# A hybrid attention and mLSTM step: the loads and the order of work ahead of the first projections

## The chip, the cores and the metric

The kernel runs on one core of a Trainium2 chip. The metric is the device time of one execution in microseconds (us), the median of several runs. In what follows PE is the tensor engine (PEld its weight loads), DVE the vector engine, ACT the scalar engine, POOL GpSimd, and SP the sync engine, which here only issues transfers (DMAs).

## The reference

One layer of a diffusion backbone. There are 128 context tokens and 1024 latent tokens, nine blocks of 128, of width 1024, all in float32. Cut to what matters here:

```python
def ada_mods(cond, w_ada_l, b_ada_l):
    m = jax.nn.silu(cond) @ w_ada_l + b_ada_l          # w_ada: 1024 x 6144
    return jnp.split(m.reshape(-1, 1, 6 * D_MODEL), 6, axis=-1)

def trunk_layer(x, mods, norm1_w, w_in, ...):
    sh1, sc1, g1, sh2, sc2, g2 = mods
    h = rmsnorm(x, norm1_w) * (1 + sc1) + sh1
    aq, ak, av, mq, mk, mv, mo, mg = jnp.split(h @ w_in, SPLIT_POINTS, axis=-1)
    ...                                                # attention beside mLSTM
    x = x + g1 * mix
    h2 = rmsnorm(x, norm2_w) * (1 + sc2) + sh2
    x = x + g2 * swiglu(h2, w_gu, w_down)
```

Context tokens are modulated by one condition vector, latent tokens by another. `w_in` is 1024 x 2832: its columns 512 to 767 give keys and values (`ak`, `av`), its last 16 the mLSTM gates (`mg`), columns 0 to 511 the queries.

## The kernel before

A Tile program: it is written as one sequence per part, and a scheduler settles at build time the order of the instructions on each engine from priorities (`hot(n)` raises them) and from its own estimate of times. Each engine then runs its instructions strictly in that order, and an instruction that waits holds up everything behind it on its engine. Products in float32 accuracy are made from splits into a high and a low half and three products: high times high, high times low, low times high.

The nine blocks are handled three at a time, as chunks c = 0, 1, 2 (`CB` = 3, `NCH` = 3); chunk c's rows lie in `x3[c]` (in the profile `x`). The part that the change touches is the start:

- **Loads.** SP issues, in this order: the identity `ident` (L117), six blocks of x (`load_x`, L308), the key, value and gate columns of `w_in` into four tiles `kraw` (two strided pieces each, L208), the 16 tiles `aw` of the columns of `w_ada` for shift (n = 0) and scale (n = 1) (L324), the last three blocks of x, the gate bias, and the four tiles `iraw` of the query columns (L208). ACT's queue issues the small vectors `crow`, `brow`, `nrow`. Every DMA from the ninth on waits for one of the eight before it to land.
- **Normalising and turning.** `normalise(c)` takes the sums of squares on ACT (L384), the root on DVE (L131 to L137), and scales the rows on DVE (L387). `turn(c)` transposes the rows on PE (L120, by the identity) and copies them back, half on ACT (L400), half on DVE (L401).
- **The scale of a weight set.** `Scaled.ready` takes the largest magnitude of a weight set on ACT (L214, `jkw`), transposes it on PE (L120), makes a power of two of it on DVE (`powers`, L176 to L179) and spreads it over the partitions on PE (L190). `pairs` splits the scaled weights into f16 halves `ipair` (L234, L235, L237, L238).
- **Shift and scale.** For each n, products of the condition with the 8 tiles `aw[n]` go to two banks, the halves j = 0, 1 (L370). Each bank is copied (`part`, L417, j = 0 on ACT, j = 1 on DVE), turned into columns (L376) and gets its bias (`modulation`, L362, L365). From both, one more power of two is made (L426 to L431).
- **Features.** `features(c)` makes the modulated rows `hT` in f16: the high half on ACT (L536), the full value on DVE (L537, four buffers `full`), their difference on DVE (L141).
- **Projections.** `linear_tok` multiplies a chunk's features by the key/value/gate weights (L512 to L514, 128x272). `evac_kvg` takes the result out on ACT (L521, L522) and the gates on DVE (L525). For c = 1 and 2 it is woven with the scale of the query weights and `ada_rest`, the products for the remaining mods (L370 with tiles `a`). After it the queries are projected (L512 to L514, 128x512).

The loop that orders the last two is short:

```python
    for c in range(NCH):
        with hot(100):
            features(c)
        prods = linear_tok(kvg_pairs, 0, 272, evac_kvg, (tuple(range(c * CB, c * CB + CB)),), bank if c == 1 else bankA)
        if c > 0:
            weave(prods, chain(steps, ada), KD, 10)
        else:
            emit(prods)
        if c == 0:
            normalise(2)
        if c == 1:
            turn(2)
```

Two loads further down play a part in the prediction: `mwh` (L771, scaled on DVE at L772), the mLSTM norm weights, and the store of `vall` (L725). After about 160 us come the mLSTM heads, the attention, the output projection and the FFN; nothing of them is touched.

## Time and profile before

| | |
|---|---|
| time, median of 3 runs (lowest to highest) | 1531.25 us (1525.82 to 1537.16) |
| profiled execution: its time, its span | 1531.07 us, 1529.3 us |
| PE busy in the span | 1473.0 us (96%) |
| DVE, ACT, POOL busy | 1015.8, 770.4, 268.8 us |
| mean granted PE clock | 0.989 of full |
| moved by DMA | 233.77 MB, mean 153 GB/s |
| PE busy in the first 45.65 us | 26.77 us |
| PE busy from 45.65 to 100 us, and from 100 to 155 us | 48.56 and 55.00 us |

The span is the profiled program from its first to its last instruction; the execution's time is some 2 us more. "PEclk" is the share of the full clock that PE was granted. In the lines of the timeline come the start and the length in us, the engine, the line of the kernel, the operation with out<-in, and in brackets the idle time just before it and what ended it. "SPq" and "ACTq" are the issuing of DMAs on these engines.

### The profile page before, as it was taken

The page shows a single profiled execution, that of the slowest core. Times are in us where ns is not written, and L with a number is a line of the kernel's source. Part 1 is how long each engine was busy: PE and PEld are TensorE (multiplying, and loading weights), DVE is VectorE, ACT ScalarE, POOL GpSimd, SP SyncE. Part 2 cuts the span into 40 slices and gives each one's busy share as a digit, 9 for nine tenths or more (in the row PEclk, how much of TensorE's full clock was granted, in tenths as well). Part 3 has the DMA queues.
Part 4 walks back from the last instruction along what each step waited for, and adds up shares of the span by engine and source line. Part 5 has one row for each costly group of instructions (what it writes and reads, how often), then busy time and mean ns, then how long its engine had stood idle before and what let it go on. Part 6 is the DMA issues. An engine that isn't in the chain of part 4 may idle for free.

```text
span 1529.3 us, 23410 instructions
## 1 busy us (share of the span) xinstructions
PE 1473.0 (96%) x8539; PEld 1244.7 (81%) x8539; DVE 1015.8 (66%) x2025; ACT 770.4 (50%) x1429; POOL 268.8 (18%) x354
## 2 busy tenths in 40 slices
PE   6899999999998899999999999999999999999997
PEld 3545567677766789999898999989998989999996
DVE  4887654838568866878637587787866585554554
ACT  4764475947654645556433444656553443323333
POOL 0113423333344441010010100100010101101110
PEclk9899999999999999999999999999999999999998
DMA  9664323523456577869635357886864445544541
GB/s 359 205 198 147 101 71 42 120 53 62 110 177 207 135 180 187 200 156 195 171 115 166 124 184 212 198 184 145 201 145 138 138 139 179 158 135 126 153 144 56
DMA packets 387113, 233.77 MB, mean 153 GB/s; under 512 B 170102, under 2 KB 347462, under 8 KB 386998
## 3 DMA queue, kind: packets, MB, share of 16 engines
q1 hardware_dynamic: 385006, 228.69, 55.0%
q10 hardware_dynamic: 1864, 3.20, 0.9%
q8 instruction: 67, 1.10, 0.3%
q14 instruction: 48, 0.39, 0.1%
q0 software_dynamic: 128, 0.39, 0.1%
HBM read 182.21 MB, written 11.69 MB: 127 GB/s over the span
## 4 chain that ended last, share of the span: by engine, by line
PE 78%; DVE 5%; DMA 3%; ACT 3%; issue 1%; POOL 1%; SPq 0%; ACTq 0%; DVEq 0%; POOLq 0%
PE mm L1437 11%; PE mm L1436 11%; PE mm L1435 11%; PE mm L1191 5%; PE mm L1192 5%; PE mm L1193 5%; PE S L1111 4%; PE wi L514 3%; PE wi L513 3%; PE wi L512 3%; PE mm L1219 2%; PE po L1136 2%; PE po L1135 2%; PE mm L1221 2%; PE mm L1223 2%
## 5 line engine op out<-in xcount | busy, mean ns | idle before, releaser
L163 ACT CAST whi<-raw 128x1024 fp32r<-128x1024 f32 x214 | 219.2, 1026 | 367.8 <-PE mm L1436 146.9
L141 DVE TENSOR_TENSOR wlo<-raw,whi 128x1024 fp32r<-128x1024 f32 x214 | 257.7, 1204 | 170.5 <-ACT whi L163 167.0
L1436 PE MATMUL mm<-aTl,whi 128*128 128x384 f32 x1056 | 354.4, 336 | 0.0
L1437 PE MATMUL mm<-aTh,wlo 128*128 128x384 f32 x1056 | 354.2, 336 | 0.0
L1435 PE MATMUL mm<-aTh,whi 128*128 128x384 f32 x1056 | 353.2, 335 | 0.0
L141 POOL TENSOR_TENSOR hl<-tn,hl 128x384 fp32r<-128x384 f32 x66 | 84.9, 1286 | 846.6 <-ACT hl L1458 796.4
L1435 PEld LDWEIGHTS mm<-aTh,whi 128*128 128x128 f32 x1056 | 198.3, 188 | 0.7
L1436 PEld LDWEIGHTS mm<-aTl,whi 128*128 128x128 f32 x1056 | 198.3, 188 | 0.6
L1437 PEld LDWEIGHTS mm<-aTh,wlo 128*128 128x128 f32 x1056 | 198.3, 188 | 0.1
L1191 PE MATMUL mm<-whi,hl 128*128 128x512 f32 x372 | 144.4, 392 | 1.1 <-DVE t L1180 1.1
L1192 PE MATMUL mm<-wlo,hl 128*128 128x512 f32 x372 | 145.1, 391 | 0.0
L1193 PE MATMUL mm<-whi,hl 128*128 128x512 f32 x372 | 142.7, 391 | 0.0
L1118 DVE SCALAR_TENSOR_TENSOR pl<-pr,st,ph 128x1152 f16<-128x1152 f32 (+1 forms) x72 | 96.9, 1346 | 37.3 <-ACT ph L1117 35.9
L1113 DVE TENSOR_REDUCE st<-S 128x1 f32<-128x1152 f32 (+1 forms) x72 | 88.9, 1234 | 17.5 <-PE S L1111 17.2
L1114 ACT ACTIVATE pr<-S,st 128x1152 f32<-128x1152 f32 (+1 forms) x72 | 81.3, 1129 | 33.0 <-DVE st L1113 28.2
L1117 ACT ACTIVATE ph<-pr,st 128x1152 f16<-128x1152 f32 (+1 forms) x72 | 83.8, 1164 | 26.3 <-issue 10.9
L1180 DVE TENSOR_TENSOR t<-mm,gl 128x512 f32<-128x512 f32 x102 | 69.1, 686 | 38.1 <-PE mm L1193 16.0
L512 PE MATMUL wi<-headw,hT 128*128 128x384 f16 x288 | 93.9, 326 | 0.2 <-ACT th L799 0.2
L513 PE MATMUL wi<-headw,hT 128*128 128x384 f16 x288 | 93.9, 326 | 0.0
L514 PE MATMUL wi<-headw,hT 128*128 128x384 f16 x288 | 93.9, 326 | 0.0
L1111 PE MATMUL S<-kst,qT 128*128 128x384 f32 (+1 forms) x400 | 84.5, 344 | 0.8 <-ACT pr L1114 0.8
L1191 PEld LDWEIGHTS mm<-whi,hl 128*128 128x128 f32 x372 | 69.9, 188 | 15.2 <-DVE t L1180 1.5
(400 smaller groups left out, 2591.3 us busy)
## 6 DMA issues: line engine op xcount, KB each, us to landing
raw<-in_w_gu_dram SPq DMA_DIRECT2D x132, 512.0 KB
raw<-in_w_down_dram SPq DMA_DIRECT2D x60, 512.0 KB
a<-in_w_ada_dram SPq DMA_DIRECT2D x24, 512.0 KB
gl<-g_d SPq DMA_DIRECT2D x36, 256.0 KB
aw<-in_w_ada_dram SPq DMA_DIRECT2D x16, 512.0 KB
iraw<-in_w_in_dram SPq DMA_DIRECT2D x32, 256.0 KB
x<-in_x_sample_dram SPq DMA_DIRECT2D x11, 512.0 KB
raw<-in_w_out_dram SPq DMA_DIRECT2D x10, 512.0 KB
```

Of the source, the lines that this page charges most:

```text
L141: (dve if eng == "dve" else pool).tensor_tensor(out=out, in0=full, in1=hi, op=ALU.subtract)
L163: nc.scalar.copy(hi[:, :n], raw[:, :n])
L512: mm(ps[:, :n], ah, wh[:, k % 2, c0 : c0 + n], start=(k == 0), stop=False)
L513: mm(ps[:, :n], ah, wl[:, k % 2, c0 : c0 + n], start=False, stop=False)
L514: mm(ps[:, :n], al, wh[:, k % 2, c0 : c0 + n], start=False, stop=(k == KD - 1))
L1111: mm(S[:, n, 0:w], qT[:, h, :], kst[kv][:, t, c0 + n * w : c0 + (n + 1) * w], start=(t == 0), stop=(t == 1))
L1191: mm(ps, ah, wh[:, k % 2, :], start=(k == 0), stop=False)
L1192: mm(ps, ah, wl[:, k % 2, :], start=False, stop=False)
L1193: mm(ps, al, wh[:, k % 2, :], start=False, stop=(k == nk - 1))
L1435: mm(ps, wh[:, k, :], th[:, k, :], start=(k == 0), stop=False)
L1436: mm(ps, wh[:, k, :], tl[:, k, :], start=False, stop=False)
L1437: mm(ps, wl[:, k, :], th[:, k, :], start=False, stop=(k == KD - 1))
```

## The change

It makes these edits, all ahead of some 100 us of the program:

1. The identity is issued by ACT's queue, ahead of the small vectors, and no longer by SP's ahead of x.
2. The key, value and gate columns of `w_in` are packed on the host into one more input, `w_kvg`, four tiles of 128 rows of 544 numbers; each `kraw` is one DMA of whole rows.
3. The tiles `aw` for scale come in two passes, first the eight left halves, then the eight right ones: 24 DMAs in all in the place of 16.
4. For scale, each half is multiplied, copied, turned and modulated before the next is begun.
5. `normalise(2)` and `turn(2)` stand ahead of chunk 1's features, with a raised priority.
6. For chunk 1, every second full value is made on ACT (L536 there) in the place of DVE.

```diff
-    dma(ident, I["k_ident"])
+    nc.scalar.dma_start(ident, I["k_ident"])
...
-    kvg = Scaled([[(lambda v: v[:, :, 0:256], rows_of(j)[:, :, 512:768]),
-                   (lambda v: v[:, :, 256:272], rows_of(j)[:, :, 2816:2832])] for j in range(4)], (2, 272),
+    kvg = Scaled([[(lambda v: v, I["w_kvg"][j])] for j in range(4)], (2, 272),
...
-    ada_w = [[], []]
-    for n in range(2):
+    ada_w = [[awp.tile([P, D], F32, name=f"aw0_{n}_{k}") for k in range(KD)] for n in range(2)]
+    for n, j, w in ((0, 0, D), (1, 0, 512), (1, 1, 512)):
         for k in range(KD):
-            aw = awp.tile([P, D], F32, name=f"aw0_{n}_{k}")
-            dma(aw, w_ada[k * P : (k + 1) * P, n * D : (n + 1) * D])
-            ada_w[n].append(aw)
+            dma(ada_w[n][k][:, j * w : (j + 1) * w], w_ada[k * P : (k + 1) * P, n * D + j * w : n * D + (j + 1) * w])
...
         halves = [bankA(), bankA()]
-        for k in range(KD):
-            for j, pe in enumerate(halves):
-                strip_products(pe, k, silp, ada_w[n][k][:, j * 512 : (j + 1) * 512], 2 * j)
-        with hot(300):
-            for j, pe in enumerate(halves):
-                part = p0.tile([P, 512], F32, name=nm("part"), tag="part", bufs=2)
-                (nc.scalar.copy if j == 0 else dve.tensor_copy)(part, pe)
-                cols_from_strips(out, n, j, part, bankA)
+        for js in ((0, 1),) if n == 0 else ((0,), (1,)):
+            for k in range(KD):
+                for j in js:
+                    strip_products(halves[j], k, silp, ada_w[n][k][:, j * 512 : (j + 1) * 512], 2 * j)
+            with hot(300):
+                for j in js:
+                    part = p0.tile([P, 512], F32, name=nm("part"), tag="part", bufs=2)
+                    (nc.scalar.copy if j == 0 else dve.tensor_copy)(part, halves[j])
+                    cols_from_strips(out, n, j, part, bankA)
...
-                dve.tensor_scalar(out=full[:, i : i + n], in0=v[:, k, i : i + n], scalar1=s, scalar2=t, op0=ALU.mult, op1=ALU.add)
+                if c == 1 and k % 2:
+                    act(full, v[:, k], AF.Identity, scale=s, bias=t)
+                else:
+                    dve.tensor_scalar(out=full[:, i : i + n], in0=v[:, k, i : i + n], scalar1=s, scalar2=t, op0=ALU.mult, op1=ALU.add)
...
     for c in range(NCH):
+        if c == 1:
+            with hot(200):
+                normalise(2)
+                turn(2)
...
-        if c == 0:
-            normalise(2)
-        if c == 1:
-            turn(2)
...
+    w = host["w_in"][0]
+    w = _np.concatenate([w[:, 512:768], w[:, 2816:2832]], 1)
+    host["w_kvg"] = w.reshape(4, 2, P, 272).transpose(0, 2, 1, 3)
```

Three places show what this does to the order. The first is ACT's queue just ahead of the first features (`hT`), before: `part` is the copy of a half of shift or scale, `jk` the squares of chunk 2's rows, `jkw` the maxima of the query weights `iraw`.

```order
L234 ACTIVATE ipair_362<-kraw_144,isc_332 128x544
L417 COPY part_383<-wi_365 128x512
L417 COPY part_417<-wi_399 128x512
L384 ACTIVATE jk_620,ssx_619<-x_2_134 128x1024
L384 ACTIVATE jk_622,ssx_619<-x_2_134 128x1024
L384 ACTIVATE jk_624,ssx_619<-x_2_134 128x1024
L214 ACTIVATE jkw,isc_689<-iraw_476 128x512
L536 ACTIVATE hT_439<-x_0_132,shift_88,scale_87 128x128
```

And with the change:

```order
L415 COPY part_387<-wi_369 128x512
L234 ACTIVATE ipair_357<-kraw_141,isc_336 128x544
L234 ACTIVATE ipair_360<-kraw_142,isc_336 128x544
L234 ACTIVATE ipair_363<-kraw_143,isc_336 128x544
L234 ACTIVATE ipair_366<-kraw_144,isc_336 128x544
L415 COPY part_413<-wi_403 128x512
L381 ACTIVATE jk_624,ssx_623<-x_2_134 128x1024
L381 ACTIVATE jk_626,ssx_623<-x_2_134 128x1024
L381 ACTIVATE jk_628,ssx_623<-x_2_134 128x1024
L214 ACTIVATE jkw,isc_729<-iraw_480 128x512 x2
L214 ACTIVATE jkw,isc_729<-iraw_481 128x512
L534 ACTIVATE hT_443<-x_0_132,shift_88,scale_87 128x128
```

The copy of the shift half has moved ahead of the four splits of the key weights, and three maxima, one of them of the second `iraw`, stand ahead of the features where there was one.

The second place is PE after chunk 1's projections, before: `isc` and `pv` belong to the scale of the query weights, `a` to the remaining mods, `x_2` is chunk 2.

```order
L514 MATMUL mm_679<-ipair_362,hT_440 128x272
L120 MATMUL mm_726<-ident,isc_689 1x128
L190 MATMUL mm_743<-pv_728,one_110 128x2
L370 MATMUL mm_772<-a_89_755,silp_473 32x256 x4
L370 MATMUL mm_772<-a_90_757,silp_473 32x256 x4
L120 MATMUL mm_804<-ident,x_2_134 128x128 x4
L370 MATMUL mm_772<-a_91_759,silp_473 32x256 x4
L120 MATMUL mm_809<-ident,x_2_134 128x128 x4
```

With the change the same work on the scale stands at the end of chunk 2's projections:

```order
L512 MATMUL wi_878<-ipair_366,hT_445 128x272
L190 MATMUL mm_783<-pv_768,one_110 128x2
L367 MATMUL mm_812<-a_95_795,silp_477 32x256 x4
L367 MATMUL mm_812<-a_96_797,silp_477 32x256 x4
L367 MATMUL mm_812<-a_97_799,silp_477 32x256 x4
L367 MATMUL mm_812<-a_98_801,silp_477 32x256 x4
L510 LDWEIGHTS hT_443
L510 MATMUL wi_1077<-ipair_1048,hT_443 128x512
```

Chunk 2's transposes have moved into chunk 0's projections, all of chunk 2's projections come next, and the first products for the remaining mods and the queries follow the scale (its transpose L120 stands eleven projections earlier).

The third place is DVE around that scale with the change: `pv` is the scale, `rt` and `ry` the root of the key norms.

```order
L186 TENSOR_REDUCE pv_768<-mm_766 1x1
L137 SCALAR_TENSOR_TENSOR ry_1120<-rt_1121,ry_1120 128x2
L135 TENSOR_TENSOR rt_1191<-ry_1190 128x8
L176 TENSOR_SCALAR pv_768<-pv_768 1x1
L135 TENSOR_TENSOR rt_1121<-ry_1120 128x2
L136 SCALAR_TENSOR_TENSOR rt_1191<-rt_1191,rv_1189 128x8
L773 TENSOR_SCALAR mwh<-mwh 128x512
L177 TENSOR_SCALAR pv_768<-pv_768 1x1
L136 SCALAR_TENSOR_TENSOR rt_1121<-rt_1121,rv_1119 128x2
L137 SCALAR_TENSOR_TENSOR ry_1190<-rt_1191,ry_1190 128x8
L577 CAST maskb<-maskf_1095 128x128
L178 TENSOR_SCALAR pv_768<-pv_768 1x1
```

The scaling of `mwh` and a cast of a mask, which both read tiles that were loaded, have moved between the pieces of the scale.

## The prediction

> **What bounds the kernel now.** I read the busy shares first, then the span cut into stretches, then the timeline of the first hundred microseconds engine by engine, then who waits for whom.
>
> The first line of the page, and the busy time of each stretch (length, then PE, PEld, DVE, ACT and POOL busy, granted clock, share of the DMA engines, GB/s):
>
> ```profile
> PE 1473.0 (96%) x8539; PEld 1244.7 (81%) x8539; DVE 1015.8 (66%) x2025; ACT 770.4 (50%) x1429; POOL 268.8 (18%) x354
> ...
> 0.00:45.65 45.65, 26.77 (x153) 15.83 (x154) 22.34 (x88) 23.55 (x52) 1.37 (x7) 0.90 0.99 365
> 45.65:100.00 54.35, 48.56 (x350) 31.66 (x351) 48.58 (x147) 38.90 (x85) 11.01 (x11) 0.89 0.63 181
> 100.00:155.00 55.00, 55.00 (x367) 26.90 (x366) 42.90 (x164) 28.72 (x52) 14.47 (x9) 1.00 0.50 160
> 155.00:160.00 5.00, 2.86 (x19) 1.77 (x18) 3.12 (x7) 3.14 (x5) 0.00 (x0) 1.00 0.77 236
> 160.00:1529.30 1369.30, 1339.78 (x7655) 1168.50 (x7653) 898.89 (x1623) 676.11 (x1237) 241.92 (x327) 0.99 0.55 144
> ```
>
> The tensor engine sets the pace, so a gain is PE idle time removed or a clock drop avoided. All edits lie in the start: from about 100 us on, every engine's order is the same in both kernels but for small swaps before 160 us. PE is idle 18.9 us before the first projection at 45.65, 5.8 us from there to 100, nothing from 100 to 155. The first 45.65 us have a floor, since the DMA engines are busy 0.99 of them. So the stake is a few microseconds of 1529, in either direction, far inside the 1% (15 us) that a measurement of this kernel can tell from no change.
>
> What releases the first projection:
>
> ```profile
> 26.61 2.66 ACT L234 ACTIVATE ipair<-kraw,isc 128x544 f16<-128x544 f32 x4 [2.63 <-DVE isc L191]
> 29.18 0.56 ACT L417 COPY part<-wi 128x512 f32<-128x512 f32 x1
> 29.80 3.48 PE L376 MATMUL wi<-strip_sel,part 128*128 128x2 f32 x16 [2.21 <-ACT part L417]
> 33.21 5.59 PE L370 MATMUL wi<-aw,silp 128*32 128x512 f32 x32
> 39.84 1.95 PE L376 MATMUL wi<-strip_sel,part 128*128 128x2 f32 x16 [1.05 <-ACT part L417]
> 41.83 0.17 DVE L362 TENSOR_TENSOR scale<-wi,bcol 128x8 f32<-128x8 f32 x1 [0.53 <-PE wi L376]
> 43.27 0.14 DVE L176 TENSOR_SCALAR pv<-pv 1x1 f32<-1x1 f32 x1
> 44.69 0.23 DVE L431 TENSOR_SCALAR scale<-scale,hsc 128x16 f32<-128x16 f32 x1
> 45.10 11.91 ACT L536 ACTIVATE hT<-x,shift,scale 128x128 f16<-128x128 f32 x24 [0.92 <-DVE shift L431]
> 45.65 0.41 PE L512 MATMUL wi<-ipair,hT 128*128 128x272 f16 x1 [1.19 <-ACT hT L536]
> ```
>
> This is one chain: the shift part waits on ACT behind four weight splits, so the products for scale start at 33.21 instead of when their weights are there, and the two halves of scale go through copy, strip sums and modulation together before the features may start.
>
> **The change part by part.** First the stream of loads. The identity leaves the sync queue, and the gate/kv weights come as four packed rows instead of eight strided pieces:
>
> ```profile
> 0.74 0.40 SPq L117 DMA_DIRECT2D ident<-in_k_ident_dram  x1
> 1.20 0.41 SPq L308 DMA_DIRECT2D x<-in_x_prompt_dram  x1
> ...
> 10.00:18.00 8.00, 4.67 (x26) 4.29 (x28) 7.08 (x33) 7.44 (x21) 0.00 (x0) 1.00 1.06 327
> 18.00:40.00 22.00, 18.58 (x109) 8.72 (x105) 10.54 (x24) 6.92 (x15) 0.60 (x1) 0.84 1.03 407
> 40.00:45.00 5.00, 2.64 (x19) 2.28 (x19) 2.50 (x18) 3.63 (x8) 0.00 (x0) 0.86 1.04 396
> ```
>
> The first x leaves 0.46 us earlier (1.20 less 0.74). While the strided pieces are under way the engines are full and move 327 GB/s instead of 407: 8 us at 80 GB/s less is 0.64 MB, or 1.6 us. The scale weights come as sixteen 256 KB pieces with rows of 2 KB instead of eight of 512 KB; the nearest row is the iraw loads after 40 us, also 2 KB rows, at 396: 4.19 MB at 396 instead of 407 is 0.3 us more. Net the stream is 0.46 + 1.6 - 0.3, about 1.7 us, ahead. The bounds are 2.1 (no cost of the split) and -0.4 (the split runs at 327, 2.5 us more). The identity on ACT's queue delays crow by about one issue (0.4 us); the transposes that need the identity start only at 13 us, and the condition's column is due when the first ada weights are there, after 17 us, so it costs nothing; without that cover it would be 0.4.
>
> The Trainium skill ("DMA: Bandwidth & Descriptors", Measured) speaks against the split: it asks for transfers of at least 1 MiB and lists 138 GB/s at 64 KB and 341 at 1 MB. This trace disagrees for several transfers in flight, since the 512 KB pieces of 18 to 40 us ran at 407; 256 KB pieces no run here shows yet.
>
> Second, the ada chain. The shift part now stands ahead of the four splits on ACT, and scale goes in two halves. Counted back from the first iraw load, which landed at 43.46 (below), with 2.1 MB (chunk 2's x, 1.57 MB, and that load, 0.52) behind the last ada weights, these were there at 43.46 - 2.1/0.407 = 38.3; now 36.6. Only one half's tail is left: the last product 0.35, the copy 0.7, half the strip sums 1.0, and 41.83 to 44.69, 2.9: the scaled shift would be ready at 41.6 instead of 44.7. But two other queues stand in the way:
>
> ```profile
> 39.69 1.06 ACT L384 ACTIVATE jk<-x 128x1024 bf16<-128x1024 f32 x1
> ...
> 43.46 0.63 ACT L214 ACTIVATE jkw<-iraw 128x512 bf16<-128x512 f32 x1 [0.55 <-DMA iraw<-in_w_in_dram]
> 44.00 0.19 ACT L214 ACTIVATION_READ_ACCUMULATOR jkw<-iraw 128x1 f32 x1
> ```
>
> On ACT three of these maxima (two of the first iraw, one of the second) now stand ahead of the features, before it was one. The second iraw lands 43.46 - 1.7 + 0.52/0.407 = 43.05; the first one's two, 0.73 each, run from 41.8 to 43.2, the third to 44.0. On DVE the root for chunk 2 now stands inside the power-scale chain and waits for that chunk's squares: landed at 40.5 (43.46 - 1.7 - 1.3), squared by 41.7, then 1.9 us of chain (43.27 to 44.69 before, and three more of 0.17), then the two scalings, 0.4: 44.0 as well. So the features start at 44.0 instead of 45.10, and **the first term is 1.1 us**, not the 3.1 of the ada chain. Its bounds: -1.0 (stream at the low bound) to 3.1.
>
> Third, what follows the start. Rows of PE by stretch, and of the two kinds of work that move:
>
> ```profile
> 45.65:53.65 8.00, 6.99 (x30) 4.19 (x31) 8.00 (x27) 8.00 (x18) 0.00 (x0) 0.50 1.11 319
> 58.60:67.10 8.50, 8.50 (x74) 6.95 (x71) 8.50 (x24) 5.89 (x20) 3.31 (x3) 1.00 0.03 9
> 67.10:69.60 2.50, 0.56 (x4) 0.36 (x3) 2.43 (x20) 1.99 (x7) 0.00 (x0) 1.00 0.01 3
> 71.00:74.40 3.40, 3.40 (x23) 1.94 (x22) 1.86 (x8) 1.58 (x3) 0.87 (x2) 0.52 0.89 286
> ...
> 67.67 0.27 PE L120 MATMUL mm<-ident,isc 128*1 128x128 f32 x1 [0.56 <-DVE isc L216]
> 69.32 0.38 PE L190 MATMUL mm<-pv,one 1*128 1x2 f32 x2 [1.38 <-DVE pv L179]
> 74.94 1.53 PE L120 MATMUL mm<-ident,x 128*128 128x128 f32 x12
> 80.11 0.64 PE L370 MATMUL mm<-a,silp 128*32 128x256 f32 x8 [0.45 <-DMA a<-in_w_ada_dram]
> ```
>
> Before, PE runs out of work at 67.1 and waits for the scale of the q weights; the clock then falls and 71.0 to 74.4 go at 0.52, 3.4 x 0.48 = 1.6 us lost. Now chunk 2's 24 transposes lie inside chunk 0's projections, and chunk 2's 72 products run on without a break, with the scale's transpose 11 products ahead of their end. PE from 44.55: 1.5 idle (1.0 as in the first row, 0.5 for DVE's normalise now between the first features), 216 products at 8.5/72 = 0.118, 25.5; 24 transposes at 0.128, 3.1; and the half clock of the first 8 us, 4.0: 78.6. DVE and ACT keep up:
>
> ```profile
> L141 DVE TENSOR_TENSOR hT<-full,hT 128x384 f16<-128x384 f32 x16 | 9.6, 621 | 0.0
> L537 DVE TENSOR_SCALAR full<-x,scale,shift 128x384 f32<-128x384 f32 x8 | 5.1, 662 | 0.0
> L387 DVE TENSOR_SCALAR x<-x,ry 128x1024 f32<-128x1024 f32 x3 | 2.1, 739 | 0.0
> L401 DVE COPY x<-mm 128x512 f32<-128x512 f32 x3 | 2.1, 691 | 2.1 <-PE mm L120 2.0
> L235 DVE SCALAR_TENSOR_TENSOR ipair<-iraw,isc,ipair 128x1024 f16<-128x1024 f32 x2 | 2.6, 1276 | 0.4 <-ACT ipair L234 0.4
> L728 DVE TENSOR_REDUCE vm<-vall 128x1 f32<-128x1280 f32 x1 | 1.5, 1475 | 0.0
> ```
>
> DVE did chunks 0 and 1 from 44.7 to 65.5, 20.8 us without a pause. To that come chunk 2's normalise and copies, 4.0 back to back, and three of its features, 1.8; four features go over to ACT, -2.4, and 1 us of the root now lies ahead of the start. That is 23 us from 43.6: 66.8. Chunk 2's other five features, eight subtractions and the gate columns are 9 us more: 76, ahead of PE's 78.6. Then PE waits for the scale: transposed at 77.3, and behind it on DVE the six small operations of the chain with as many of the key's norm and the 128x512 mwh scaling between them, some 2.6 us: 79.9, a gap of 1.4 where it was 2.5. The 16 ada products (2.1) and four with the high part (0.9) lead to 83.3; the low part needs DVE's 1.5 (vm) and 1.2 (ipair) and is there at 84.1: 0.8. With 0.9 for what I can't place, PE's idle time is 1.5 + 1.4 + 0.8 + 0.9 = 4.6 where it was 5.8: **the second term is 1.2 us**. The gap being shorter than the one that brought the clock down, **the third term is the 1.6 us**; if it falls again the term is 0.
>
> The Trainium skill ("TensorE: Matmul & The Clock Gate", HAM oscillation) lets the clock fall only after idle gaps over about 3.4 us. The rows above show it fall after 2.5 us with 0.56 us of small matmuls in them, so the row decides here; by the page alone 1.4 us would be safe with more room.
>
> Last, whether the gain lasts. PE is full from 100 to 155 and idles 2.1 us behind one wait:
>
> ```profile
> PE wi L849 <- ACT qraw L754: 2.1, 1, 2.1
> ```
>
> The norms that lead to it start from q products that move with PE, so I carry the gain through whole. The sum is 1.1 + 1.2 + 1.6 = 3.9 us off the profiled execution, whose own time is 1531.07, 0.2 below the median of the three runs: **1527.2 us**, 0.3% faster.
>
> **The rivals.** (1) Nothing is left: DVE and ACT are full from 45 to 57 and the extra 4.0 us of chunk 2's work there delays PE, while the gap at the end of chunk 2 is as long as the old one and the clock falls too. The second term becomes -0.5 and the third 0: 1530.5. For it: 8.00 of 8.00 on both engines. Against it: chunk 2's end comes from PE's sum, not DVE's.
> (2) Slower, on one wait: the mwh scaling on DVE now lies between the pieces of the scale chain, and DVE stops there until that load lands; PE's L190 and everything behind it (ada products, all q products) stand still. It decides against the change once DVE waits over 2.3 us, since the clock's 1.6 goes too. A wait of 5 us gives 3.9 - 1.6 - 5 = 2.7 lost: 1533.8. For it: the load is issued behind the store of vall, which waits for ACT. Against it: that store was issued at 59 us, some 18 us ahead.
> (3) The split is slow after all, the rule of the page on transfer sizes, here as 4.19 MB at the strided pieces' 327 GB/s: the start is 1.0 late instead of 1.1 early: 1529.3. The 407 of the 512 KB pieces speaks against it.
> (4) More: the clock recovers sooner, PE having less idle time ahead of the features: 4.0 us more at most, 1523.2. Against it: PE still has only some 3 us of work in the last 8 ahead of them.
>
> **How the numbers follow.** I give my forecast 0.42, (1) 0.25, (2) 0.13, (3) 0.10, (4) 0.10. The time is the forecast's. The range goes from 1521 to 1535: the rivals' 1523.2 to 1533.8, and some 2 us on each side, because the runs of the kernel before alone spread from 1525.8 to 1537.2. No case reaches 1% on either side. I leave 0.03 for a gain over 1% (the idle time of the whole start would have to go), 0.04 for a loss over 1% (a wait like (2) of 17 us or more), 0.93 for within.
>
> **What would show it.** Right: the rate stays near 400 GB/s from 10 to 18 us; the first L510-L512 product (L512 to L514 now) starts near 44.6, released by ACT; ACT waits for an iraw load just ahead of its features; no clock drop after 58 us; the gap ahead of the scale's L190 is under 2 us; the order from 100 us on is 3 to 5 us earlier. Wrong: features that start at 42 (then the two queues don't gate), a second stretch at 0.5 clock near 80, a DVE wait on mwh, or a stretch from 100 to 160 us that takes back what was won.

## The result and the profile after

The changed kernel takes 1527.3 us (median of 22 runs, 1524.0 to 1530.9) against 1531.7 us (22 runs, 1525.8 to 1537.2) in the same session: the ratio is 0.9974, with a 95% interval from 0.9964 to 0.9983. That is 4.0 us less by the ratio, where 3.9 were forecast. The profiled execution took 1524.74 us with a span of 1523.0, near the low end of the 22 runs and 6.3 us less than the profiled execution before. So the size was right (by the interval, 2.6 to 5.5 us less), and 0.3% can be told from no change here, finer than the 1% that the prediction allowed a measurement. The way to it was not in all its steps.

The page's first line after, and the same stretches as before (length, then PE, PEld, DVE, ACT and POOL busy, granted clock, share of the DMA engines, GB/s):

```profile
PE 1466.2 (96%) x8539; PEld 1239.4 (81%) x8539; DVE 1017.2 (67%) x2021; ACT 771.3 (51%) x1433; POOL 268.0 (18%) x354
...
0.00:45.65 45.65, 26.25 (x153) 14.19 (x153) 22.80 (x95) 24.35 (x55) 1.31 (x7) 0.94 0.97 363
45.65:100.00 54.35, 49.39 (x370) 32.16 (x371) 46.87 (x150) 42.82 (x92) 12.90 (x12) 0.95 0.60 172
100.00:155.00 55.00, 53.11 (x364) 26.50 (x362) 46.19 (x155) 28.17 (x52) 12.76 (x8) 1.00 0.61 193
155.00:160.00 5.00, 5.00 (x34) 3.09 (x31) 4.74 (x13) 4.86 (x14) 0.00 (x0) 1.00 0.51 158
...
70.00:75.00 5.00, 5.00 (x46) 4.23 (x44) 5.00 (x16) 3.17 (x11) 0.05 (x1) 1.00 0.02 5
```

From 45.65 to 100 us PE is busy 49.39 instead of 48.56 us, and at 0.95 of the clock instead of 0.89; the stretch near 70 us, at 0.52 before, now runs at full clock. From 100 to 155 PE idles 1.9 us where it idled nothing, and from 155 to 160 it idles nothing where it idled 2.1. In the first 45.65 us nothing was won. The timeline there:

```profile
38.87 1.06 ACT L381 ACTIVATE jk<-x 128x1024 bf16<-128x1024 f32 x1 [5.01 <-DMA x<-in_x_sample_dram]
...
40.72 0.17 DVE L362 TENSOR_TENSOR scale<-scale,ncol 128x8 f32<-128x8 f32 x1
...
42.78 0.17 DVE L131 TENSOR_SCALAR rv<-ssx 128x3 f32<-128x3 f32 x1 [0.85 <-ACT jk L381]
...
43.30 0.63 ACT L214 ACTIVATE jkw<-iraw 128x512 bf16<-128x512 f32 x1 [0.55 <-DMA iraw<-in_w_in_dram]
...
44.67 0.34 DVE L538 TENSOR_SCALAR full<-x,scale,shift 128x128 f32<-128x128 f32 x1
...
45.44 1.85 ACT L534 ACTIVATE hT<-x,shift,scale 128x128 f16<-128x128 f32 x4
45.97 0.41 PE L510 MATMUL wi<-ipair,hT 128*128 128x272 f16 x1 [2.03 <-ACT hT L534]
```

The two queues hold the features up as foreseen: DVE's root (L131) waits for chunk 2's squares, and ACT goes through three maxima before its first feature. But the first iraw lands at 43.30, only 0.16 us ahead of the 43.46 before, so the first projection is at 45.97, 0.3 us later than before and 1.4 later than forecast. The first of the head products, an order that both kernels share, shows what is left of it all:

```profile
L849 PE MATMUL wi<-hT,headw x96: 322/326/336, 158.2 to 381.6; 128*128 128x384 f16 x96
```

before, and after:

```profile
L850 PE MATMUL wi<-hT,headw x96: 323/326/336, 153.3 to 376.6; 128*128 128x384 f16 x96
```

It starts 4.9 us earlier and ends 5.0 us earlier. The other 1.3 us of the profiled 6.3 arose later, in work that the change doesn't touch. The likely reason, not tested, is the clock: 13 of the 14 executions profiled here have one to three drops of it between 270 and 530 us, and this one has none.

### The profile page after: what moved, and what is told of

Its sections match the earlier page's. It is cut to its first block, busy times and chain, and to the rows that moved or that the text cites. A ratio compares the mean times of both kernels' runs of the same rounds, so it can differ in the third digit from the quotient of the medians.

```text
span 1523.0 us, 23411 instructions
## 1 busy us (share of the span) xinstructions
PE 1466.2 (96%) x8539; PEld 1239.4 (81%) x8539; DVE 1017.2 (67%) x2021; ACT 771.3 (51%) x1433; POOL 268.0 (18%) x354
## 4 chain that ended last, share of the span: by engine, by line
PE 59%; DVE 2%; DMA 1%; ACT 0%; issue 0%; SPq 0%; DVEq 0%
PE mm L1438 11%; PE mm L1437 11%; PE mm L1436 11%; PE mm L1192 5%; PE mm L1193 5%; PE mm L1194 5%; PE S L1112 3%; PE po L1137 1%; PE po L1136 1%; DMA plT<-pl 1%; PE mm L1224 1%; PE mm L1220 1%; PE mm L1222 1%; DVE t L1181 0%; DVE x L1182 0%; PE mm L120 0%
```

## The experiments

Ratios are to the kernel before, measured beside it. Each interval is about 0.0013 wide to either side (2 us), so two kernels that differ by 2 us are not quite told apart (the interval of such a difference is 2 to 3 us to either side); the traces carry more than the times.

**The load stream alone.**

```diff
# on the kernel before
+    nc.scalar.dma_start(ident, I["k_ident"])            # was dma(...)
+    kvg = Scaled([[(lambda v: v, I["w_kvg"][j])] ...    # packed on the host
```

> The kernel before with edits 1 and 2 alone: the identity on ACT's queue, the key, value and gate weights packed. By the prediction's first term the stream is 2.1 us ahead: 393 GB/s or more from 10 to 18 us, the last of the scale weights landing near 36.2 instead of 38.3, the second modulation at 39.8 instead of 41.8. Four maxima of iraw stand ahead of the features here, so they start when the second iraw tile has landed and been read, 44.0 to 44.4, and the first projection near 44.8 instead of 45.65. Chunk 2 is still transposed behind chunk 1, so the idle stretch ahead of the query scale and the clock drop near 70 us stay as in the kernel before if the drop is a matter of that gap. Time: 0.8 below the kernel before (1530.9), at most 2.1 below. If the stream is not ahead in the end because something later takes it back (the rival), the second modulation is at 41 or later and the time that of before.

Measured: 1531.03 us, ratio 1.0003 (0.9992 to 1.0014). Two stretches of its stream:

```profile
24.00:34.00 10.00, 9.63 (x63) 4.39 (x63) 5.22 (x16) 3.83 (x6) 0.00 (x0) 0.83 1.03 407
...
38.50:41.00 2.50, 1.95 (x16) 1.86 (x16) 0.72 (x5) 2.50 (x6) 0.00 (x0) 0.98 1.06 405
```

and of its timeline:

```profile
40.74 0.17 DVE L364 TENSOR_TENSOR scale<-scale,ncol 128x8 f32<-128x8 f32 x1
...
41.56 0.63 ACT L214 ACTIVATE jkw<-iraw 128x512 bf16<-128x512 f32 x1
...
45.04 0.41 PE L511 MATMUL wi<-ipair,hT 128*128 128x272 f16 x1 [1.19 <-ACT hT L535]
```

The same two stretches of the changed kernel:

```profile
24.00:34.00 10.00, 8.58 (x56) 4.20 (x56) 5.21 (x15) 4.42 (x7) 0.00 (x0) 0.83 1.05 385
38.50:41.00 2.50, 1.20 (x9) 0.97 (x8) 1.19 (x5) 2.05 (x3) 0.00 (x0) 1.00 0.72 223
```

The packing does what the first term said: the second modulation is done 1.3 us earlier than before (40.74 for 42.03), the first iraw is read at 41.56 instead of 43.46, the first projection starts 0.6 us earlier. In the changed kernel that lead is lost again: 385 instead of 407 GB/s over 10 us (0.5 us), and a hole at 38.5 to 41 us, 223 instead of 405 (1.1 us). And a lead at the start brought no time by itself.

What was expected further down did not come. Chunk 2 is still turned behind chunk 1, but the gap ahead of the products that follow the query scale is only 1.0 us, and the clock does not fall near 70 us:

```profile
69.78 1.89 PE L369 MATMUL mm<-a,silp 128*32 128x256 f32 x26 [0.97 <-DVE isc L191]
```

So this kernel starts 0.6 us earlier and has no drop near 70 us, and still its time is that of the kernel before. This bears on the third term of the prediction (below).

**Whole loads for scale, and the gate on ACT.** The first kernel puts ACT's maxima behind the features, the second also loads the scale weights whole again.

```diff
         with hot(100):
             features(c)
+            if c == 0:
+                nc.scalar.copy(jkw[:, 0:1], hTh[0][:, KD - 1, 0:1])
```

```diff
# the second one also
-    for n, j, w in ((0, 0, D), (1, 0, 512), (1, 1, 512)):
+    for n, j, w in ((0, 0, D), (1, 0, D)):
```

> The changed kernel with one small ACT copy into the maxima's scratch tile behind chunk 0's last feature, so that ACT's maxima of the query weights all stand behind the features. Theory G (the gate on ACT set the start): the features start when DVE has scaled shift and scale, which was 44.5 us in the changed kernel, so the first projection starts near 45.0 instead of 45.97, and since that microsecond lies in the stretch at half clock the time falls by 0.5 to 1.0 us against the changed kernel, to about 1526.6. Theory S (the stream of loads set it, through chunk 2's x, whose squares stand ahead of the features on ACT and whose root stands inside DVE's chain): the features start at 44.4 to 44.7 and no earlier, since DVE still waits for the squares at 42.8. If the first projection stays at 45.9, both are wrong. In either case the transpose and the gap ahead of the query scale stay at 1 to 2 us.

> As the kernel before it in this list, and the scale weights come whole again, eight loads of 512 KB instead of sixteen of 256 KB (their products still go half by half). Theory S: the stretch from 24 to 34 us runs at 405 to 410 GB/s instead of 383, worth 0.6 us, the hole from 38.5 to 41 us (113 to 256 GB/s, worth 1.1 us) closes, and the last iraw load lands 1 to 1.7 us earlier; chunk 2's squares end near 41.3 and DVE scales near 43.2. Rival (the split cost nothing; the hole is that of the gate bias's 64-byte rows and stays): the stretch stays at 383 to 390 and the squares end at 42.4 or later. The products of scale's left half can't start before all weights of both halves are there, so the second modulation may be no earlier than 40.5. Sixteen transposes of chunk 2 stand ahead of the first projection in this order, so the first projection is late by up to 2 us and tells nothing by itself. Time within 2 us of the changed kernel's, 1525 to 1529.

Measured: 1528.94 us, ratio 0.9990 (0.9979 to 1.0001), and 1530.75 us, ratio 1.0001 (0.9990 to 1.0013). Both miss. Of the first, what PE waited for:

```profile
PE mm L190 <- DVE ry L137: 5.1, 1, 5.1
```

(us in total, times, the longest), and of its stretches:

```profile
80.00:85.00 5.00, 1.28 (x10) 0.90 (x14) 4.27 (x24) 0.49 (x1) 1.12 (x2) 0.77 0.27 66
```

The first projection did not come earlier (46.26), because in this execution PE ran at half clock from 31.5 to 52 us and the ada chain with it; and the maxima, once behind, ran so late that the query scale kept PE waiting 5.1 us and the clock fell. So the maxima ahead of the features were no loss on balance: they pay for the short gap later. In the second, the stream ran at 407 GB/s in both stretches, as with whole loads in the kernel above: the halves go with the lower rate, and the deep hole was seen only with them. Its order of transposes was another one and its time tells nothing more.

**The gate bias.**

```diff
-    dma(gbias, ...)          # ahead of the iraw loads
     next(steps)              # issues the iraw loads
+    dma(gbias, ...)
```

> The changed kernel with one load moved: the gate bias (128 rows of 64 bytes) is issued behind the four iraw loads instead of ahead of them; every other order stays. In the kernels with halved scale loads the stream showed a hole from 38.5 to 41 us (113 to 290 GB/s) while those small rows went through, in the kernels with whole loads it didn't (405). Theory S (the hole is these rows meeting a queue that holds too little): the rate stays near 400 from 38.5 to 41, the first iraw lands near 42.2 instead of 43.3, the third x before 40.5, ACT's maxima end a microsecond sooner and the first projection starts near 45.0 instead of 45.97; time 1526.3 to 1526.8. Rival (the hole comes from the halves alone): it stays where it is, first projection at 45.9, time 1527.3.

Measured: 1526.49 us, ratio 0.9972 (0.9957 to 0.9987). In its stretches:

```profile
38.50:41.00 2.50, 1.61 (x11) 0.58 (x3) 0.77 (x2) 2.21 (x5) 0.00 (x0) 0.50 1.04 406
...
30.45:54.35 23.90, 17.88 (x78) 9.30 (x73) 13.72 (x56) 14.90 (x33) 0.00 (x0) 0.50 0.98 339
```

and in its timeline:

```profile
41.51 0.63 ACT L214 ACTIVATE jkw<-iraw 128x512 bf16<-128x512 f32 x1
...
42.52 0.17 DVE L362 TENSOR_TENSOR scale<-scale,ncol 128x8 f32<-128x8 f32 x1
...
45.71 0.34 DVE L538 TENSOR_SCALAR full<-x,scale,shift 128x128 f32<-128x128 f32 x1
...
80.41 0.35 PE L190 MATMUL mm<-pv,one 1*128 1x2 f32 x2 [1.33 <-DVE rt L135]
```

The hole is gone (406 GB/s), and the maxima start at 41.51: with the halves, it was the 128 rows of 64 bytes of the gate bias that made it. Why they cost more behind the smaller loads, no run here shows. The features start no earlier all the same: scale is ready only at 42.52, because PE ran at half clock from 30.45 to 54.35 us. The time came out as expected, but the first projection did not (46.24 instead of 45.0), and the time isn't told apart from the changed kernel's, so the agreement says little.

**The clock.** What separates these executions shows in one kernel's rows. The changed kernel:

```profile
33.48:43.72 10.24, 6.26 (x35) 3.01 (x35) 2.95 (x18) 4.24 (x8) 0.00 (x0) 1.00 0.96 358
43.72:50.54 6.82, 4.48 (x20) 2.48 (x20) 6.75 (x29) 6.76 (x18) 0.00 (x0) 0.50 1.08 370
```

Half clock comes in multiples of 3.41 us, from 3.4 to 23.9 us in these executions, on a grid that lies elsewhere in each. Up to the features the order of work is nearly the same in nine of the profiled kernels. In five of them the clock stayed at half from 30 to 31.5 us on until 47.7 or later; in four it was back by 33.5 or 38.4, or had not fallen before 43. In the first group scale is ready at 42.1 to 42.6 us, in the second at 39.9 to 40.7. In four of the nine, the changed kernel and those without edit 5, without edit 6 and with the maxima behind, the loads and the order of PE's products up to the first projection are the same, one for one; two of them fell in each group. So it is the execution and not the edit that decides, and the ada chain loses or wins some 2 us by it. The Trainium skill ("TensorE: Matmul & The Clock Gate", What's actually happening) says that the activity window is 3413 ns long and free-running, so that the number of slow products varies from run to run; these traces agree, with pieces of 3.41 us and its multiples.

**Holding the clock.**

```diff
+    filler(3, "strip")       # 128x128 by 128x272 products, read by nobody
     ...
+        filler(5, "turned")
     ...
+        filler(8, "spread")
```

> The changed kernel with sixteen extra products on PE whose results nobody reads (128x128 by 128x272, f16): three behind the strip sums of scale's second half, five behind the transpose of the bound, eight behind the spread of its power, all in time in which PE idled (40.3 to 46 us). Every other order stays. Theory C (PE's clock falls after 43 us because PE has so little to do from 40 to 46, and the length of that half clock is what separates fast from slow executions): the half clock after 43 us shrinks from 6.8 to 13.7 us to at most 3.4, and since each 3.4 us of it holds 1.6 to 1.7 us of lost work the time falls by 1.5 to 3 us, to 1524.3 to 1525.8. Rival D (DVE, busy 5.00 of 5 us from 45 to 85, sets the pace of the features in this stretch, so a faster PE only waits more): PE's waits for hT on DVE grow by what the clock gives, and the time stays within 0.5 us of 1527.3. If the extra products don't hold the clock, nothing moves either, but the clock shows it.

Measured: 1528.2 us, ratio 0.9980 (0.9967 to 0.9993). In its stretches:

```profile
30.59:47.66 17.07, 14.98 (x67) 7.72 (x61) 7.20 (x39) 8.38 (x19) 0.00 (x0) 0.50 1.03 378
...
55.00:60.00 5.00, 3.55 (x28) 2.44 (x26) 5.00 (x8) 4.77 (x10) 4.70 (x5) 1.00 0.42 87
```

and in its timeline:

```profile
45.72 0.34 DVE L550 TENSOR_SCALAR full<-x,scale,shift 128x128 f32<-128x128 f32 x1
...
80.42 0.35 PE L190 MATMUL mm<-pv,one 1*128 1x2 f32 x2 [1.33 <-DVE rt L135]
```

In the kernel with the later gate bias, the stretch to set beside it:

```profile
55.00:60.00 5.00, 5.00 (x46) 4.45 (x45) 5.00 (x8) 4.77 (x10) 4.71 (x5) 1.00 0.41 90
```

Its time was not the 1524.3 to 1525.8 of theory C; it is 0.9 us above the 1527.3 of rival D, within the interval. The traces say more, and this is the clearest pair of the study. Both kernels start their features on DVE at 45.7. In one the clock is back at 47.7, in the other at 54.35, 6.7 us later; and yet the query scale is spread at 80.42 in the one and 80.41 in the other, released by DVE in both. What the clock gave, PE spent waiting for DVE (1.45 us idle from 55 to 60). That is what rival D (theory D from here on) says: DVE, which pauses for 0.1 us at most from 45 to 85, sets the pace up to there. In the changed kernel the distance from DVE's first full value to that product is the same: 79.21 less 44.67 is 34.5, here 34.7 twice. The row of that product in the changed kernel:

```profile
79.21 0.35 PE L190 MATMUL mm<-pv,one 1*128 1x2 f32 x2 [1.33 <-DVE rt L135]
```

**Chunk 1's full values back on DVE, and chunk 2 back in its old place.**

```diff
# the first: without edit 6
-                if c == 1 and k % 2:
-                    act(full, v[:, k], AF.Identity, scale=s, bias=t)
-                else:
                     dve.tensor_scalar(out=full[:, i : i + n], ...
```

```diff
# the second: without edit 5
-        if c == 1:
-            with hot(200):
-                normalise(2)
-                turn(2)
...
+        if c == 0:
+            normalise(2)
+        if c == 1:
+            turn(2)
```

> The changed kernel without edit 6: the four full values of chunk 1 that ACT made are DVE's again, 4 x 0.6 = 2.4 us more on DVE between 55 and 75 us. By the prediction's sum (DVE would be done at 76 against PE's 78.6 with the edit) PE's end moves by nothing to 0.5 us, since DVE ends at about the same time as PE then: 1527.3 to 1527.8. Rival D (DVE sets the pace from 45 to 85 us already): the whole 2.4 us show up at the end of chunk 2's projections, 77.9 becomes about 80, and the time is 1529.0 to 1529.7.

> The changed kernel without edit 5: chunk 2 is normalised behind chunk 0's projections and turned behind chunk 1's, as before. If terms two and three are what edit 5 brought, PE again runs dry behind chunk 1's projections ahead of the query scale (2 us or more with only small products in it), the clock may fall to half for 3.4 us near 70 us, and the time is 1.2 to 2.8 us above the changed kernel's: 1528.5 to 1530.1. Rival (the gain is the half clock at the start being shorter, and has nothing to do with edit 5): the time stays at 1527.3 and the half clock after 45 us lasts to about 50.5 here too.

Measured: 1528.07 us, ratio 0.9986 (0.9974 to 0.9997), and 1529.65 us, ratio 0.9988 (0.9976 to 1.0000). Of the first:

```profile
43.86 0.34 DVE L535 TENSOR_SCALAR full<-x,scale,shift 128x128 f32<-128x128 f32 x1
...
80.22 0.38 PE L190 MATMUL mm<-pv,one 1*128 1x2 f32 x2
```

The distance is 36.4 instead of 34.5 to 34.7 (PE, held up by the features on the way, comes to that product without a wait): 1.7 to 1.8 of the 2.4 us of work show on the path, most of what theory D says, and not the 0 to 0.5 of the prediction's sum. The time lies between the two forecasts. By the ratios, edit 6 is worth 1.8 us and edit 5 2.1, each with an interval of some 2.3 us to either side, so neither is told from nothing by the times alone. Without edit 5 the clock drops again, from 61.9 to 65.3 us:

```profile
60.00:65.00 5.00, 3.63 (x20) 2.27 (x18) 5.00 (x12) 4.31 (x14) 2.26 (x3) 0.69 0.05 13
...
61.73 0.73 PE L512 MATMUL mm<-ipair,hT 128*128 128x272 f16 x3 [1.37 <-DVE hT L141]
71.88 0.35 PE L190 MATMUL mm<-pv,one 1*128 1x2 f32 x2 [1.60 <-DVE pv L179]
```

But this drop comes behind waits for features (1.37 us), ten microseconds ahead of the query scale. The gap ahead of the scale is there too (1.60 us), and behind that one the clock did not fall.

**The kernel before, once more.**

> The kernel before unchanged, profiled a second time, to see what of its clock is the kernel's and what the execution's. If the drop near 70 us is caused by the gap ahead of the query scale (the third term of the prediction), it is there again, as 3.4 us at half clock that begin within 3.4 us of the gap. If such drops are a matter of where a grid of 3.4 us happens to fall, it may be missing, and the half clock after 43 us may be 6.8 or 13.7 us long instead of 10.2. Time within 1526 to 1537.

Measured: 1533.5 us (one run). Its half clock:

```profile
44.15:54.39 10.24, 7.58 (x32) 4.57 (x33) 9.74 (x42) 9.04 (x21) 0.00 (x0) 0.50 0.98 301
71.45:74.87 3.42, 3.42 (x27) 1.51 (x18) 1.90 (x14) 2.50 (x3) 0.87 (x2) 0.50 0.59 195
```

The drop behind chunk 1 is there again, half a microsecond from where it was, and so is the gap ahead of it (1.39 us at the scale). So it is no matter of the one execution. What the gap has to do with it shows when each profile is cut along its own grid of 3.41 us. Of the kernel before, the piece just ahead of the drop, and of the kernel without edit 5 the piece with its gap, behind which the clock stayed up:

```profile
67.47:70.88 3.41, 1.83 (x21) 1.04 (x22) 3.31 (x31) 2.57 (x7) 0.00 (x0) 1.00 0.01 2
68.73:72.14 3.41, 1.81 (x16) 1.35 (x13) 1.86 (x12) 2.18 (x7) 0.85 (x2) 1.00 0.08 22
```

In the fourteen profiles, all 35 falls between 52 and 1513 us follow a piece in which PE was busy for 1.86 us or less (1.16 us ahead of the drop in this second profile). But 27 such pieces at full clock were not followed by a fall. A gap that leaves PE idle for about half a piece can bring the clock down; whether it does is partly chance, also because the grid can split it.

**Edits 5 and 6 alone.**

```diff
# on the kernel before; the two old places of chunk 2 go
+        if c == 1:
+            with hot(200):
+                normalise(2)
+                turn(2)
...
+                if c == 1 and k % 2:
+                    act(full, v[:, k], AF.Identity, scale=s, bias=t)
```

> The kernel before with edits 5 and 6 alone: chunk 2 normalised and turned ahead of chunk 1's features, and chunk 1's odd full values on ACT. The loads and the ada chain are as before. Theory E (the gain is the idle time and the clock drop behind chunk 1, nothing of it comes from the loads): the drop near 70 us is gone, PE's idle time from 45.65 to 100 us is about 1.2 us shorter, and the time is 1527.5 to 1528.5, as far below the kernel before as the changed kernel. Rival (the loads and the half chain carry part of it): 1529 to 1530. A time at 1531 would say that the edits work only together.

Measured: 1528.1 us, ratio 0.9981 (0.9967 to 0.9995): 2.9 of the 4.0 us without any edit of the loads or the ada chain. For whom PE waited:

```profile
PE mm L120 <- DVE x L387: 4.0, 1, 4.0
```

and the stretch behind it:

```profile
60.00:65.00 5.00, 3.25 (x15) 3.25 (x16) 5.00 (x8) 2.95 (x10) 2.28 (x3) 0.67 0.20 66
```

In its own order PE waits 4.0 us for chunk 2's rows, the clock falls near the end of that wait and again at 89 us, and PE idles 7.3 us from its first projection to 100 us, not some 1.2 less than the 5.8 of before. So the time came as expected but not the way to it, and it is no clean sum of two parts. What the four edits of the start add, 1.1 us, is within the intervals.

**Less work on DVE.** Three kernels, each on the one before: eight differences go to POOL (with the later gate bias); then extra products on PE; then the reduction of the values behind the first low half of the query weights.

```diff
-            sub(hl[:, k], full, hh[:, k], "dve")
+            sub(hl[:, k], full, hh[:, k], "pool" if c > 0 and k % 2 else "dve")
```

```diff
+    filler(3, "strip") ... filler(5, "turned") ... filler(4, "spread")
```

```diff
+        with behind("low"):        # the first low half of the query weights
             dve.tensor_reduce(out=vm[:, 0:1], in_=vall, ...)
```

> The changed kernel with the gate bias issued behind iraw (as in the earlier run) and with eight of the differences for the low halves of the features (odd k of chunks 1 and 2) on POOL instead of DVE: 8 x 0.62 = 5.0 us less on DVE between 50 and 80 us, about 10 us more on POOL, which has 6 us to do there. Theory D (DVE's work from the features' start to the end of chunk 2's projections, 33.3 us in three runs whatever PE's clock was, sets the pace): the projections of chunk 2 end 1 us earlier or more, counted from the start of DVE's features (32.3 or less instead of 33.2 to 33.4), the gap ahead of the query scale shrinks since DVE's small operations no longer queue behind features, and the time falls by 1 to 2 us against the changed kernel, to 1525.3 to 1526.3. Rival (PE's own sum, 28.6 us of work plus half of what runs at half clock, sets it): the end stays within 0.3 us of 33.3 where the half clock lasts beyond 50 us, and the time stays at 1526.5 to 1527.3.

> The kernel before it in this list with twelve extra products on PE whose results nobody reads (three, five and four at the three places of the earlier run), to shorten the half clock. If DVE and PE are about equally long from 45 to 80 us, so that taking away only the one or only the other gave nothing, both together must show: the half clock ends by 47.7 as in the earlier run with extra products, the projections of chunk 2 end 31 to 32 us after the start of DVE's features instead of 33.3, and the time falls to 1524.5 to 1525.5. If the time stays at 1526 to 1527, neither engine's work there sets the end, and what comes behind (the query scale, the loads of a, the split of the query weights) does.

> The last kernel but one (gate bias behind iraw, eight differences on POOL, twelve extra products) with one more order: the reduction vm over the values (1.47 us on DVE) goes behind the first low half of the query weights instead of ahead of it. PE waited 2.41 us for that half there. If DVE's order behind the query scale sets the pace now, that wait falls to about 1.0 and the time by 1.0 to 1.4 us, to about 1523.8; it would be the fastest of all. Rival (the second low half or the loads of a wait next): the 1.4 us come back within the next 20 us, the first head product is at the same distance from the first query product as before plus 1.4, and the time stays at 1525.0.

Measured: 1525.23 us, ratio 0.9962 (0.9949 to 0.9976); 1525.01, ratio 0.9964 (0.9949 to 0.9978); 1522.47, ratio 0.9943 (0.9926 to 0.9960). Of the first:

```profile
45.27 0.34 DVE L538 TENSOR_SCALAR full<-x,scale,shift 128x128 f32<-128x128 f32 x1
```

and of its stretches:

```profile
65.00:70.00 5.00, 5.00 (x44) 4.22 (x44) 4.15 (x12) 5.00 (x13) 0.97 (x2) 1.00 0.22 66
...
100.00:115.00 15.00, 15.00 (x106) 6.56 (x105) 10.28 (x37) 7.39 (x15) 3.55 (x3) 1.00 0.65 203
```

The time fell as forecast, but not where: chunk 2's projections ended 34.1 us after DVE's start, not 32.3 or less. DVE now has pauses (4.15 of 5), and PE, at half clock to 53.9 us here, was last. The gain lies from 100 to 115 us, where PE idles nothing, against 1.55 us in the changed kernel:

```profile
100.00:115.00 15.00, 13.45 (x98) 5.52 (x96) 11.64 (x43) 6.12 (x14) 4.43 (x3) 1.00 0.63 203
```

In the changed kernel those are a wait of 0.8 us for a load of the remaining mods and one of 0.7 us for DVE. With the gate bias moved alone PE still waits 2.7 us from 100 to 116 us, so it isn't that edit by itself; more was not settled. With the extra products the projections ended after 33.0 us, short of the forecast, and the time was the same. The wait for the low half in that kernel:

```profile
83.12 0.38 PE L523 MATMUL wi<-ipair,hT 128*128 128x512 f16 x1 [2.41 <-DVE ipair L235]
```

And of the last kernel, two rows:

```profile
77.75 0.35 PE L190 MATMUL mm<-pv,one 1*128 1x2 f32 x2 [0.89 <-DVE rt L136]
81.95 0.38 PE L525 MATMUL wi<-ipair,hT 128*128 128x512 f16 x1 [1.02 <-DVE ipair L235]
```

PE's wait for the low half fell from 2.41 to 1.02 us, as forecast. But the first head product is 70.1 and 70.0 us behind the first query product in the two, so in the profile the 1.4 us came back, and whether the 2.5 us between the two medians are more than chance is open. Against the kernel before and the changed kernel this last version is faster beyond the intervals: some 8.7 and 4.7 us.

## Why the prediction was right, and where it was not

The total held: 3.9 us forecast for the profiled execution, 4.0 by the ratio. In part that is luck: by its own terms as measured, -0.3, 1.2 and at most 1.6 make 2.5, and the profiled executions differ by 6.3. Of the signs of being right that it named, only the first product near 44.6 us failed to come. Rivals 1 and 2 fell: the time went down, and the scaling of mwh ran on DVE without a wait. Of rival 3 a part came true, a start 0.3 us late instead of its 1.0.

**First term, 1.1 us: wrong, it was -0.3 by the first projection.** The step that failed is "Net the stream is 0.46 + 1.6 - 0.3, about 1.7 us, ahead". The packing was sized nearly right (393 GB/s from 10 to 18 us where it was 327, 1.3 of the 1.6 us, and the kernel with the loads alone had the lead). The split was not: the halves ran at 385, not at the 396 taken from the iraw rows, and the gate bias, which the sum left out, cost 1.1 us behind them. The page on transfers that the prediction weighed (the Trainium skill, "DMA: Bandwidth & Descriptors", Measured) had the direction right, smaller is slower, and the sizes not: 256 KB at 385 GB/s and 512 KB at 407, issued by SP with several in flight, lie above the 341 that it lists for 1 MB issued from GpSimd. The bounds of the split, 327 to 407, held it; the choice in between did not, and the hole was outside the step altogether. The two queues that gate the features were read rightly. But the ACT gate is no cost on balance: with the maxima behind the features PE waited 5.1 us for the query scale instead of 1.3. And where DVE sets the pace, its own start counts: its first full value comes at 44.67 instead of 45.11 us, 0.4 early, while ACT and PE start 0.3 late.

**Second term, 1.2 us: right in sum.** PE's idle time from the first projection to 100 us is 4.6 us (54.35 less 49.39, less the 0.32 ahead of 45.97), as forecast. The gap ahead of the query scale is 1.33 us (forecast 1.4), the wait for the low half 1.24 (0.8); the rest leans on the 0.9 us that the prediction could not place. The reason given for it was wrong: "DVE and ACT keep up", DVE done at 76 ahead of PE's 78.6. The product with the scale was released by DVE in the changed kernel and in the pair above, at a fixed distance from DVE's start, whether PE was fast or slow; and 2.4 us more on DVE showed as 1.7 to 1.8. Taking 5.0 us off DVE brought chunk 2's end no nearer, so the two engines are about equally long there, and PE's sum came out right because of that.

**Third term, 1.6 us: the drop went, its price is not shown.** The drop at 71 to 75 us was there in both profiles of the kernel before and is gone in the changed kernel, where PE is busy for 2.08 us in the piece with the gap. But two other kernels with chunk 2 in its old place have none there either, the one with the loads alone and the one without edit 5. They do the same products between the query scale and the first query product, in a slightly different order. The stretches, of the kernel before, of the loads alone and without edit 5:

```profile
69.32:85.49 16.17, 15.16 (x135) 9.45 (x135) 13.75 (x49) 11.42 (x17) 4.32 (x4) 0.89 0.82 263
68.43:85.03 16.60, 15.07 (x136) 9.29 (x135) 13.74 (x52) 12.98 (x23) 3.84 (x4) 1.00 0.72 222
71.88:87.00 15.12, 14.22 (x135) 8.69 (x135) 12.65 (x41) 11.43 (x17) 4.50 (x2) 1.00 0.82 260
```

With the drop it takes 16.2 us, at full clock 16.6 and 15.1. By these kernels the drop cost between nothing and 1.1 us there, not 1.6. Nor does an early chunk 2 alone keep the clock up: without edit 6 it fell from 86.2 to 89.6 us, behind a wait of 1.91 us for the low half.

**What the sum did not have:** the half clock ahead of 50 us was taken as fixed at 4.0 us. It lasted 6.8 us from 43.7 here and 10.2 in both profiles of before, and in the nine kernels of nearly the same order it ended anywhere from 48 to 54 us. This is rival 4's mechanism, most likely by chance and not by the change. The pair of kernels above shows that it moved the query scale by nothing; what it can move is the ada chain, by some 2 us.

**Whether the gain lasts:** yes, 4.9 us at the first head product, though the wait for the norms (2.1 us) gave way to 1.9 us of new idle time earlier.

## What to carry to other kernels

When two engines are busy without a pause through a stretch, add up both from the same start and ask what releases the last instruction; the one whose work you move may be the one that sets the end. Give a load that is made smaller its own rate and look at what queues behind it: a few rows of 64 bytes cost a microsecond there. In a kernel like this one a single profile's clock below 100 us is a draw: compare landmarks, such as the distance between two instructions, over several executions before a microsecond is put down to an edit.

## What the hardware showed unexpectedly

- 128 rows of 64 bytes in the queue cut the stream to 223 GB/s for 2.5 us where the loads of scale ahead of them were 256 KB each (213 to 312 in the five kernels of that kind). Where those were 512 KB it was 360 to 407 in five others, and with the small rows issued last 404 to 406.
- Loads of 256 KB with rows of 2 KB ran at 385 GB/s, those of 512 KB with rows of 4 KB at 407.
- The clock fell to half behind a wait of 1.82 us near 515 us in the profiled execution before, and did not behind the same wait of 1.82 us near 510 us in the one after (PE busy for 1.60 and 1.71 us in the piece of 3.41 us that holds the wait). Nor did work without a pause always bring it back: with the maxima behind the features PE was busy for all of 34.9 to 38.3 us, with the ada products, and stayed at half.
